# Bidirectional RWKV layer ahead of latent attention: the scan's operands at 1.7 parts per stretch instead of 2.4, the POOL work beside its inverses on DVE, and the first two attention weight tiles in a pool of their own

## The chip, the cores and the metric

One core of one Trainium2 chip runs the whole program in one launch. The metric is the device time of one execution in microseconds; the time before is 4227.73 us, the median of 3 runs (4226.45 to 4228.69). The engines are called PE (TensorE, matmuls), DVE (VectorE), ACT (ScalarE), POOL (GpSimd) and SP (the queue from which most DMAs are issued).

## The reference, cut to what matters

The network has two blocks. The first (two hybrid attention layers with their feed-forward parts) is not touched. The second has four layers on 512 tokens and 256 context tokens, 1024 wide: a gated mixer, an RWKV-7 layer, latent attention, and a gated mixer again. The change lies in the RWKV layer and at the start of the latent attention.

```python
def rwkv7_scan(state0, r, decay, k_dir, v, kk, a, emit):
    ...
    def step(S, inp):
        w_t, k_t, v_t, kk_t, a_t = inp[:5]
        s_kk = jnp.einsum('nbhvk,nbhk->nbhv', S, kk_t)
        S = S * w_t[..., None, :] - s_kk[..., :, None] * (kk_t * a_t)[..., None, :] + v_t[..., :, None] * k_t[..., None, :]
        y_t = jnp.einsum('nbhvk,nbhk->nbhv', S, inp[5]) if emit else None
        return S, y_t
    ...
    y = ys[0] + jnp.flip(ys[1], axis=1)

def rwkv7_output(y, r, k_dir, v, z, r_k, ln_gain, ln_bias, w_out):
    ...
    yn = ((yh - mean) * lax.rsqrt(var + RWKV_LN_EPS)).reshape(y.shape) * ln_gain + ln_bias
    ...
    out = (yn + jnp.sum(bonus, axis=0).reshape(y.shape)).astype(z.dtype)
    return (out * jax.nn.silu(z)) @ w_out

def mla_project(h, w_in, q_norm, kv_norm, w_uq, w_ukv, qk_gain_q, qk_gain_k, need_q):
    ...
        c_q, c_kv, k_rope, z = jnp.split(h @ w_in, [...], axis=-1)
```

The scan runs over 768 tokens (the context's state feeds the latent tokens) in two directions, for 16 heads of 64.

## The kernel before, in words

**Precision.** A full-precision product is three passes (`strip`, L160): each weight tile `wraw` is split into a high part `whi` (L138, ACT) and a low part `wlo` (L141, on DVE, and on POOL at every third tile), and the activations likewise (`split`, L177 on ACT and L178).

**The order of work.** PE's instructions stand in the order in which the Python generators emit them. DVE, ACT, POOL and SP are ordered ahead of time by a scheduler in the compiler, and then each runs its list strictly in order, so an instruction that waits holds everything behind it on its engine.

**The features of the RWKV layer** (`features`). PE makes 32 strips: the eight 128-wide tiles of k, then r, z and v. A strip is eight contraction tiles of 512 + 256 columns and is cut in four stretches; a stretch has pace 1, in the two strips where one kind gives way to the next 0.4. Beside the strips run four side generators, each with a rate: the lora products, `operands` (rate `OPS`, L1185), `by_tokens` and `first`. After each stretch a generator earns its rate times the stretch's pace, and for each whole credit it emits one part.

**The operands.** `operands(f)` (L1571) exists for f = 0 to 7, one for every two heads, and is about 16 parts. A part early on emits the products of the decay and rate loras on PE (L1603, read by ACT in L1604) and the norm's rows (L1264). Then for each of the two directions: kd (L1618, POOL), L1619 and the running sum L1625 (DVE), the exponentials (ACT), and the tiles `st_bk` and `st_ar` (L1645 on POOL, L1646, L1647 and L1649 on DVE), written to DRAM. Some parts later `within` (L1668) multiplies them on PE (L1679) and stores the 32 x 32 blocks that `inverse` reads. `by_tokens(f)` waits until operand set f is done.

**The inverses.** `inverse(k)` (k = 0 to 7, one for each operand set) inverts 96 triangular blocks of 32 x 32 in 31 steps of two instructions (L1819, L1821). `first` (L1473) runs inverse 0 on DVE beside the v strips, then `merge(0)`; when all operand sets are done it closes their pool, makes the masks and starts inverse 1 on POOL. Inverses 2 to 7 follow on POOL during the scan. Each ends with stores to DRAM (L1829), which `merge(k)` (L1832) reads back into `TT`; its first matmuls are L1854.

**The scan.** For each k, 12 steps (`step`, L1885 to L1920) form one period; within period k the products and the merge of k + 1 and the output of k - 1 are interleaved on PE. `output` (L1933) normalises `yacc`, adds `ld_b` on POOL (L1959), multiplies by the gate on DVE (L1961), splits it (L177 on ACT, L178 on POOL) and multiplies by two 128 x 512 tiles of `rwkv_w_out_2`. In `step`, DVE copies `rh` (L1892) and the lower half of `VU`, updates `st` (L1908) and writes `SV` (L1915), each between two small matmuls.

**The latent attention's start** (`Mla.run`). A weight pool is opened for the projections; the first two weight tiles `wkv` (128 x 1024) are asked from it ahead of the layer's normed input `hidden` (L978, L979), and the first strip uses both.

Of the kernel before, what the change touches and what calls it, by code (L numbers as in the profile page):

```python
# [16 lines left out]
ALU = mybir.AluOpType  # L17
# [1099 lines left out]
CH = 64  # L1117
# [64 lines left out]
OW = (0.0, 0.4, 1.0)  # L1182
BANKS = (4, 4)
PACE = 0.4
OPS = 2.4  # L1185
WT = 3


class Rwkv:
# [32 lines left out]
    def work(self, tag, shape, bufs, k=0):  # L1222

        at = {"T12": 1, "TT": (3, 2, 0)[k % 3]}.get(tag)
        if at is None:
            return (self.op if tag[:3] == "inv" and tag != "invW" else self.ap).tile(shape, F32, tag=tag, name=tag, bufs=bufs)
        return shaped(self.big(at), shape)
# [247 lines left out]
    def first(self):  # L1475

        tc = self.net.tc
        while self.done["xs"] != "v":
            yield
        self.cur = cur = [{} for k in range(KD)]  # L1480
        X = [self.big(2), self.big(3)]
        cut = lambda t, a, n: t[:, a:a + n]
        place = {"invA": [cut(X[0], 0, 1024)], "invT": [cut(X[1], 0, 1024)], "invP": [cut(X[0], 1024, 256)]}
        turn = {}

        def work(tag, shape, bufs, k=0):
            if tag == "T12":
                return self.work(tag, shape, bufs, k)
            turn[tag] = turn.get(tag, -1) + 1
            return shaped(place[tag][turn[tag] % len(place[tag])], shape)  # L1490

        acc = self.net.aux
        for _ in self.inverse(0, cur[0], work, self.net.nc.vector):
            yield
        t = self.big(2)
        place = {"invW": [cut(t, 768, 256), cut(t, 1024, 256)], "TT": [self.big(3)]}
        yield from self.merge(0, cur[0], work, acc)

        while self.done["op"] < KD:
            yield  # L1500
        self.right.close()
        self.op = self.right.enter_context(tc.tile_pool(name="rwc", reuse_waits="tile", bufs=1, side="right"))
        self.masks(self.op.tile([128, 2, 64], F32, name="rmask"))
        self.slot, self.groups, self.gs = 0, 0, []
        self.steps_to_come = self.ahead(cur)
        inv = self.inverse(1, cur[1], self.work, self.net.nc.gpsimd)
        for _ in range(9):
            next(self.steps_to_come)
            for _ in range(2):
                next(inv)  # L1510
                yield
        yield from inv
# [319 lines left out]
    def merge(self, k, cur, work, acc):  # L1832

        net, nc, ap = self.net, self.net.nc, self.ap
        mt = cur["mt"]
        TA = cur["TT"] = work("TT", [128, 2, NS, CH], 1, k)
        T12 = work("T12", [128, 2, 24, 32], 1)
        T1, M = T12[:, 0], T12[:, 1]
        TF = TA.rearrange("p d s t -> p (d s) t")
        for e in range(2):  # L1840
            nc.sync.dma_start(M[64 * e:64 * e + 32], self.mo[k][e])
            nc.sync.dma_start(T1[64 * e:64 * e + 32], self.blocks(mt[1], e, 0))
            for h in range(2):
                q = 64 * e + 32 * h
                nc.sync.dma_start(TF[q:q + 32, :, 32 * h:32 * h + 32], self.blocks(mt[0], e, h))
            nc.gpsimd.memset(TF[64 * e + 32:64 * e + 64, :, 0:32], 0.0)
        for _ in range(8):
            yield
        for g in range(3):
            pw = acc()  # L1850
            for x in range(8):
                for e in range(2):
                    a, bq = slice(64 * e, 64 * e + 32), slice(64 * e + 32, 64 * e + 64)
                    nc.tensor.matmul(pw[bq, x * 32:x * 32 + 32], lhsT=M[a, g * 8 + x, :], rhs=T1[a, g * 8 + x, :],  # L1854
                                     start=True, stop=True, tile_position=(64 * e, 64 * e + 32))
            yield
            W = work("invW", [128, 8, 32], 2)
            for e in range(2):
                bq = slice(64 * e + 32, 64 * e + 64)
                nc.scalar.copy(W[bq].rearrange("p a b -> p (a b)"), pw[bq, :256])  # L1860
            yield
            pz = acc()
            for x in range(8):
                for e in range(2):
                    a, bq = slice(64 * e, 64 * e + 32), slice(64 * e + 32, 64 * e + 64)
                    nc.tensor.matmul(pz[a, x * 32:x * 32 + 32], lhsT=W[bq, x, :], rhs=TF[bq, g * 8 + x, 32:64],
                                     start=True, stop=True, tile_position=(64 * e + 32, 64 * e))
            yield
            for e in range(2):
                a = slice(64 * e, 64 * e + 32)  # L1870
                nc.scalar.activation(TF[a, g * 8:g * 8 + 8, 32:64], pz[a, :256].rearrange("p (x c) -> p x c", c=32), AF.Copy, scale=-1.0)
            yield
# [60 lines left out]
    def output(self, k, cur):  # L1933
# [22 lines left out]
        yield  # L1956
        nc.scalar.activation(y, y, AF.Identity, scale=col(P["lg"], k), bias=col(P["lb"], k))
        yield
        nc.gpsimd.tensor_tensor(y, y, bonus, ALU.add)  # L1959
        yield  # L1960
        nc.vector.scalar_tensor_tensor(y, y, 0.5, z, ALU.mult, ALU.mult)  # L1961
        yield
        yh = ap.tile([128, T], F32R, tag="yh", name="yh", bufs=1)
        yl = ap.tile([128, T], F32R, tag="yl", name="yl", bufs=1)
        net.split(yh, yl, y, nc.gpsimd)
        yield
        for f in range(KD):
            if f % 4 == 0:
                hi, lo = net.wtile([(0, net.I["rwkv_w_out_2"][0][rows, f * 128:f * 128 + 512])], 1, 512)
            a, b = net.acc(), net.acc()  # L1970
            outs = [(a, 0, S), (b[:, :C], S, T)]
            net.strip(outs, [(hi[:, 0], lo[:, 0])], [(yh, yl)], c0=f % 4 * 128)
            yield
            self.b2.residual(self.i, f, outs, ap if k == KD - 1 else None)
# [22 lines left out]
class Mla:  # L1997
# [5 lines left out]
    def run(self):  # L2003
# [5 lines left out]
        with ExitStack() as es:  # L2009
# [24 lines left out]
            krt = mp.tile([128, NT2, 64], F32, name="krt")  # L2034
            kr2 = mp.tile([128, NT2], F32, name="kr2")
            with net.weight_pool(2, 3, 2), net.psum(6, 2), tc.tile_pool(name="mla1", reuse_waits="tile", bufs=3) as ap:
                wkv = [net.wcols(w_in[:, 768 + k * 128:896 + k * 128], 128) for k in range(2)]
                hT = self.b2.hidden(i, ap, ap, True)

                raw = [ap.tile([128, T], F32, name=f"ckr{k}", bufs=1) for k in range(2)]  # L2040
# [28 lines left out]
                for h in range(MH):  # L2069
                    ps = net.acc()  # L2070
                    net.strip([(ps, 0, S)], net.wcols(w_in[:, 1088 + h * 128:1216 + h * 128], 128), hT)
                    z = ap.tile([128, S], F32, tag="zs", name="zs", bufs=2)
                    nc.scalar.activation(z, ps, AF.Tanh, scale=0.5)
                    nc.vector.scalar_tensor_tensor(z, z, 1.0, ps, ALU.add, ALU.mult)
                    nc.sync.dma_start(zd[h * 128:h * 128 + 128, :], z)
                    if h == 0:
                        self.normed(rawq, cq, cols["qn"], 768, ((0, NCH),), ap)
            net.drop_context()
            na, nb, nw, no = HEAD_BANKS
            with net.weight_pool(1, 3, 3), net.psum(na, nb, nw), tc.tile_pool(name="po", reuse_waits="tile", bufs=no, space=PSUM) as self.pv, \  # L2080
# [382 lines left out]
```

## Time and profile before

| What | Before |
|---|---|
| Median of 3 runs | 4227.73 us |
| Profiled execution | 4218.81 us |
| Its span | 4216.9 us |
| Mean granted TensorE clock | 0.952 |
| PE busy | 3855.6 us, 91% of the span, 26432 matmuls |
| DVE busy | 2461.7 us, 58% |
| ACT busy | 1545.2 us, 37% |
| POOL busy | 1317.8 us, 31%, 1340 instructions |

The profiled execution lies 8.9 us below the median of the runs. A busy share is a mean over the whole program; the changed places lie between 2134 us and 3092 us of the span, where the share differs from stage to stage. In the rows below, a time is counted from the start of the span, and the granted clock (PEclk) is a share of full speed, averaged over the stretch.

### The profile page before, as it was taken

Reading aid. Unit: us, or ns where it says so; the run is one execution under the profiler, and the core shown is the slowest. Engines: PE = TensorE matmul, PEld = TensorE weight load, DVE = VectorE, ACT = ScalarE, POOL = GpSimd, SP = SyncE. Lnnn points to the kernel's source line nnn. Section 1 sums busy time; section 2 is a strip of 40 time slices with the busy share of each in tenths; the row PEclk is TensorE's granted clock in tenths of the full one; section 3 lists DMA queues with packets and bytes.
Section 4 is the critical chain, followed back from the end, with each engine's and each line's share of the span. In section 5 each row is a group of like instructions: output and inputs, shape, how many; then the busy total and the mean of one; then the engine's idle time right before and its main releaser. Section 6 shows DMA issues by size and latency. Waiting matters only on the chain. (4 is left out here: it accounts for less than half of the span.)

```text
span 4216.9 us, 67232 instructions
## 1 busy us (share of the span) xinstructions
PE 3855.6 (91%) x26432; PEld 3192.2 (76%) x26432; DVE 2461.7 (58%) x4804; ACT 1545.2 (37%) x2945; POOL 1317.8 (31%) x1340
## 2 busy tenths in 40 slices
PE   8999999999999999998887797588789899998999
PEld 7867777787877788887766576477577788887887
DVE  7836445865554434444767644477643778883544
ACT  4243223334332422223454433244343455553222
POOL 3321111322111211113445578820121344442221
PEclk9999999999999999999899898799889999999999
DMA  3125543213364322222257866355223121221332
GB/s 92 51 79 162 175 132 90 61 56 100 103 202 158 102 65 61 60 61 78 70 158 202 226 166 156 91 128 124 79 61 114 51 61 52 61 77 62 93 91 85
DMA packets 599015, 431.72 MB, mean 102 GB/s; under 512 B 193436, under 2 KB 532140, under 8 KB 598700
## 3 DMA queue, kind: packets, MB, share of 16 engines
q1 hardware_dynamic: 593756, 414.97, 34.1%
q0 software_dynamic: 4944, 12.46, 1.2%
q8 instruction: 209, 3.42, 0.3%
q14 instruction: 106, 0.87, 0.1%
HBM read 354.46 MB, written 68.68 MB: 100 GB/s over the span
## 5 line engine op out<-in xcount | busy, mean ns | idle before, releaser
L138 ACT CAST whi<-wraw 128x1024 fp32r<-128x1024 f32 (+3 forms) x471 | 457.5, 972 | 1183.0 <-PE acc L160 971.4
L141 POOL TENSOR_TENSOR wlo<-wraw,whi 128x1024 fp32r<-128x1024 f32 (+2 forms) x205 | 426.9, 2083 | 1291.3 <-ACT whi L138 1182.1
L160 PE MATMUL acc<-hh,whi 128*128 128x512 f32 (+2 forms) x1776 | 625.2, 377 | 9.5 <-ACT hh L421 5.0
L160 PE MATMUL acc<-hl,whi 128*128 128x512 f32 (+2 forms) x1776 | 620.8, 374 | 2.5 <-DVE hl L422 2.5
L160 PE MATMUL acc<-hh,wlo 128*128 128x512 f32 (+2 forms) x1776 | 620.3, 374 | 2.0 <-DVE wlo L141 2.0
L141 DVE TENSOR_TENSOR wlo<-wraw,whi 128x1024 fp32r<-128x1024 f32 (+3 forms) x266 | 330.6, 1244 | 467.1 <-ACT whi L138 420.7
L160 PEld LDWEIGHTS acc<-hh,whi 128*128 128x128 f32 (+1 forms) x1776 | 314.7, 188 | 84.0 <-ACT whi L138 17.3
L160 PEld LDWEIGHTS acc<-hh,wlo 128*128 128x128 f32 (+1 forms) x1776 | 314.4, 187 | 63.4 <-DVE wlo L141 2.8
L160 PEld LDWEIGHTS acc<-hl,whi 128*128 128x128 f32 (+1 forms) x1776 | 314.6, 188 | 62.3 <-DVE hl L422 4.1
L160 PE MATMUL acc<-wlo,hh 128*128 128x256 f32 (+1 forms) x896 | 297.2, 332 | 6.5 <-DVE wlo L141 6.5
L160 PE MATMUL acc<-whi,hh 128*128 128x256 f32 (+1 forms) x896 | 298.1, 335 | 2.9 <-ACT hh L978 2.3
L160 PE MATMUL acc<-whi,hl 128*128 128x256 f32 (+1 forms) x896 | 293.4, 331 | 1.5 <-DVE hl L979 1.5
L999 DVE SCALAR_TENSOR_TENSOR xT<-acc,mod,xT 128x512 f32<-128x512 f32 x256 | 185.6, 746 | 139.6 <-PE acc L160 138.9
L160 PEld LDWEIGHTS acc<-wlo,hh 128*128 128x128 f32 x896 | 179.5, 201 | 20.4 <-DVE wlo L141 7.3
L160 PEld LDWEIGHTS acc<-whi,hh 128*128 128x128 f32 x896 | 179.4, 201 | 20.5 <-ACT hh L978 2.9
L160 PEld LDWEIGHTS acc<-whi,hl 128*128 128x128 f32 x896 | 178.4, 200 | 16.3 <-DVE hl L979 2.4
L160 PE MATMUL wide<-xsh,whi 128*128 128x512 f32 (+1 forms) x512 | 147.4, 371 | 16.5 <-ACT xsh L1384 16.5
L160 PE MATMUL wide<-xsl,whi 128*128 128x512 f32 (+1 forms) x512 | 142.0, 360 | 17.0 <-POOL xsl L1385 13.5
L160 PE MATMUL wide<-xsh,wlo 128*128 128x512 f32 (+1 forms) x512 | 140.0, 356 | 0.0
L160 PE MATMUL acc<-ffgh,whi 128*128 128x512 f32 x352 | 139.9, 400 | 0.0
L160 PE MATMUL acc<-ffgl,whi 128*128 128x512 f32 x352 | 138.4, 395 | 0.0
L160 PE MATMUL acc<-ffgh,wlo 128*128 128x512 f32 x352 | 138.3, 395 | 0.0
(625 smaller groups left out, 8754.9 us busy)
## 6 DMA issues: line engine op xcount, KB each, us to landing
ada_w<-in_ada_w SPq DMA_DIRECT2D x32, 1536.0 KB
wraw<-in_sgu_w_in SPq DMA_DIRECT2D x96, 512.0 KB
wraw<-in_w_up SPq DMA_DIRECT2D x88, 512.0 KB
wraw<-in_w_in SPq DMA_DIRECT2D x44, 512.0 KB
wraw<-in_w_down SPq DMA_DIRECT2D x32, 512.0 KB
wraw<-in_sgu_w_out SPq DMA_DIRECT2D x32, 512.0 KB
wraw<-in_rwkv_w_in SPq DMA_DIRECT2D x32, 512.0 KB
bk<-rw_bk SPq DMA_DIRECT2D x24, 512.0 KB
```

The source lines that it names most:

```text
L138: nc.scalar.copy(hi, raw)
L141: eng.tensor_tensor(lo, raw, hi.bitcast(F32), ALU.subtract)
L160: mm(out, lhsT=a, rhs=b[:, t0:t1], start=first and n == 0, stop=last and n == 2)
L999: nc.vector.scalar_tensor_tensor(dst[k], ps, m[:, 16 + k, j:j + 1], dst[k], ALU.mult, ALU.add)
```

## The change

1. `OPS` goes from 2.4 to 1.7, so the 128 or so parts of the eight operand sets are spread over more stretches of the features.
2. In `output`, three uses of POOL become uses of DVE: the sum with `ld_b` (L1959), the low part `yl` (L178), and the low parts of the two weight tiles (`nc_lo`), five of sixteen of which stood on POOL.
3. `merge` cleared two pieces of a new `TT` with POOL for every k (L1846, 16 memsets); now three tiles are kept in turn and cleared once each, on DVE.
4. The attention's two first weight tiles come from a pool of their own, "mlw", on the right side of the memory, which is closed after the projections.

```diff
-OPS = 2.4
+OPS = 1.7
...
         self.cur = cur = [{} for k in range(KD)]
+        self.tts = []
...
-        TA = cur["TT"] = work("TT", [128, 2, NS, CH], 1, k)
+
+        if k < 3:
+            self.tts.append(work("TT", [128, 2, NS, CH], 1, k))
+        TA = cur["TT"] = self.tts[k % 3]
...
-            nc.gpsimd.memset(TF[64 * e + 32:64 * e + 64, :, 0:32], 0.0)
+            if k < 3:
+                nc.vector.memset(TF[64 * e + 32:64 * e + 64, :, 0:32], 0.0)
...
-        nc.gpsimd.tensor_tensor(y, y, bonus, ALU.add)
+        nc.vector.tensor_tensor(y, y, bonus, ALU.add)
...
-        net.split(yh, yl, y, nc.gpsimd)
+        net.split(yh, yl, y)
...
-                hi, lo = net.wtile([(0, net.I["rwkv_w_out_2"][0][rows, f * 128:f * 128 + 512])], 1, 512)
+                hi, lo = net.wtile([(0, net.I["rwkv_w_out_2"][0][rows, f * 128:f * 128 + 512])], 1, 512, nc_lo=nc.vector)
...
+                own = net.wp, net.wbufs
+                early = ExitStack()
+                net.wp, net.wbufs = early.enter_context(tc.tile_pool(name="mlw", reuse_waits="tile", bufs=1, side="right")), (1, 2, 2)
                 wkv = [net.wcols(w_in[:, 768 + k * 128:896 + k * 128], 128) for k in range(2)]
+                net.wp, net.wbufs = own
...
+            early.close()
             net.drop_context()
```

A line of the changed kernel has a number that is 1 to 11 higher than in the kernel before. The first place where the order moves is POOL at the start of inverse 1. Before, the list reads as follows (`st_bk` is the last operand set's, `rmask` and `G` belong to the scan's masks, `xsl` is an activation's low part for a v strip):

```order
L1645 TENSOR_TENSOR st_bk<-kd,tmp 128x12x64
L1233 MEMSET rmask 128x128
...
L1812 MEMSET invT 96x1024
L1385 TENSOR_TENSOR xsl<-xs,xsh 128x768
L1813 MEMSET invT 96x32
L1385 TENSOR_TENSOR xsl<-xs,xsh 128x768
L1813 MEMSET invT 96x32
L1819 TENSOR_TENSOR invP<-invA,invT 96x31
L141 TENSOR_TENSOR wlo<-wraw,whi 128x1024
L1821 TENSOR_TENSOR invT<-invT,invP 96x31
```

Now the same place reads:

```order
L1646 TENSOR_TENSOR st_bk<-kd,tmp 128x12x64
L1233 MEMSET rmask 128x128
L1761 MEMSET G_20323 64x8x64 x2
L1811 DMA invA<-rw_md_16218 96x1024
L1813 MEMSET invT 96x1024
L1237 AFFINE_SELECT rmask<-rmask 64x64 x4
L1811 DMA invA<-rw_md_16219 96x1024
L1813 MEMSET invT 96x1024
L1814 MEMSET invT 96x32 x2
L1820 TENSOR_TENSOR invP<-invA,invT 96x31
L1822 TENSOR_TENSOR invT<-invT,invP 96x31
```

The `xsl` and `wlo` instructions no longer stand between the steps of an inverse: the last operand set comes after the last `xsl`, and from there on POOL's list is the seven inverses one after the other.

The second place is DVE during inverse 0. Before, only two `wlo`, the copies `rst` and the inverse's own steps stand in it; now the last operand sets do too:

```order
L1822 TENSOR_TENSOR xx_19351<-xx_19351,xx_19350 96x5x27
L1647 TENSOR_TENSOR st_ar<-eb,ld_r 128x12x64
L1820 TENSOR_TENSOR xx_19350<-xx_19350,xx_19351 96x112
L1822 TENSOR_TENSOR xx_19351<-xx_19351,xx_19350 96x4x28
L1820 TENSOR_TENSOR xx_19350<-xx_19350,xx_19351 96x87
L1822 TENSOR_TENSOR xx_19351<-xx_19351,xx_19350 96x3x29
L1820 TENSOR_TENSOR xx_19350<-xx_19350,xx_19351 96x60
L1611 SCALAR_TENSOR_TENSOR kq<-ld_k,col_rwkv,aux 128x512
L1611 SCALAR_TENSOR_TENSOR kq<-ld_k,col_rwkv,aux 128x256
```

Here `xx` is inverse 0's working tile, and L1611 and L1647 belong to the last operand sets; before, all L1611 and L1647 of the eight sets stood ahead of the first step of inverse 0.

The third place is the first output of the scan. On POOL before, its two instructions stand inside inverse 6 (13x19 and so on are the sizes of its steps):

```order
L1821 TENSOR_TENSOR invT<-invT,invP 96x13x19
L1819 TENSOR_TENSOR invP<-invA,invT 96x240
L1959 TENSOR_TENSOR yacc<-yacc,ld_b 128x768
L1821 TENSOR_TENSOR invT<-invT,invP 96x12x20
L1819 TENSOR_TENSOR invP<-invA,invT 96x231
L1821 TENSOR_TENSOR invT<-invT,invP 96x11x21
L178 TENSOR_TENSOR yl<-yacc,yh 128x768
```

On DVE now, between the small instructions of the scan's steps:

```order
L1960 TENSOR_TENSOR yacc<-yacc,acc 128x512
L1960 TENSOR_TENSOR yacc<-yacc,acc 128x256
L1903 COPY VU<-aux 64x2x64
L1964 TENSOR_TENSOR yacc<-yacc,ld_b 128x768
L1903 COPY VU<-aux 64x2x64
L1913 SCALAR_TENSOR_TENSOR st<-st,rw_ec,aux 128x64 x2
L1966 SCALAR_TENSOR_TENSOR yacc<-yacc,ld_z 128x768
L1920 TENSOR_TENSOR SV<-st,rw_ec 64x2x64
L1913 SCALAR_TENSOR_TENSOR st<-st,rw_ec,aux 128x64 x2
L1920 TENSOR_TENSOR SV<-st,rw_ec 64x2x64
L178 TENSOR_TENSOR yl<-yacc,yh 128x768
```

L1964 and L178 are the two that stood on POOL; the gate's product (L1961 before, L1966 now) stood and stands on DVE behind the sum with `ld_b`.

## Rows read from the trace of the kernel before

**Rows 1.** Busy time by stage: microseconds, engines' busy time, granted clock, DMA.
```profile
core 0: us, PE busy (x) PEld busy (x) DVE busy (x) ACT busy (x) POOL busy (x), PEclk, DMA share, GB/s
2134.00:2407.00 273.00, 212.47 (x1682) 171.76 (x1681) 191.75 (x160) 140.17 (x211) 139.62 (x83) 0.91 0.75 203
2407.00:2541.00 134.00, 114.43 (x813) 94.33 (x812) 65.75 (x104) 38.08 (x66) 104.75 (x168) 0.91 0.67 184
2630.00:2735.00 105.00, 52.79 (x887) 43.80 (x887) 43.34 (x129) 22.77 (x70) 92.81 (x163) 0.72 0.39 88
2795.00:2957.00 162.00, 144.65 (x2652) 119.55 (x2650) 119.92 (x387) 68.62 (x211) 16.38 (x12) 0.98 0.54 127
3041.00:3092.00 51.00, 26.11 (x109) 21.02 (x109) 27.32 (x67) 18.64 (x31) 16.19 (x15) 0.64 0.17 52
```

**Rows 2.** Lines of PE, 2134 to 2407 us: busy, mean ns, idle before them.
```profile
line engine op names shapes xcount | busy us, mean ns | idle before us <-releasers
L1679 PE MATMUL aux<-st_ar,st_bk 64*64 64x64 f32 x768 | 32.6, 252 | 40.6 <-DVE st_bk L1647 40.6
L1603 PE MATMUL aux<-ha,a 64*128 64x512 f32 (+1 forms) x64 | 15.0, 515 | 4.0 <-ACT tmp L1604 4.0
L1603 PE MATMUL aux<-hw,w 64*128 64x512 f32 (+1 forms) x64 | 14.9, 589 | 0.0
L1264 PE MATMUL aux<-ident,hs_rep 128*128 128x128 f32 x48 | 9.2, 328 | 15.9 <-ACT tmp L1604 15.9
```

**Rows 3.** Lines of DVE, 2407 to 2541 us: the steps of inverse 0.
```profile
L1821 DVE TENSOR_TENSOR xx<-xx,xx 96x31 f32<-96x31 f32 (+15 forms) x31 | 17.9, 578 | 1.0
L1819 DVE TENSOR_TENSOR xx<-xx,xx 96x31 f32<-96x31 f32 (+15 forms) x31 | 17.4, 563 | 1.0
```

**Rows 4.** Waits by engine, 2630 to 2735 us: total, times, longest.
```profile
engine line waited for: us in total, times, longest us
PE aux L1885 <- DVE rh L1892: 44.3, 1, 44.3
ACT yh L177 <- DVE yacc L1961: 44.3, 1, 44.3
DVE yacc L1961 <- POOL yacc L1959: 43.1, 1, 43.1
```

**Rows 5.** Timeline of that wait's end: start, duration, instruction, idle before.
```profile
start us, us, engine line op out<-in xcount [idle before <-releaser]
2691.78 1.80 POOL L1959 TENSOR_TENSOR yacc<-yacc,ld_b 128x768 f32<-128x768 f32 x1
2693.61 1.43 DVE L1961 SCALAR_TENSOR_TENSOR yacc<-yacc,ld_z 128x768 f32<-128x768 f32 x1 [43.12 <-POOL yacc L1959]
2695.30 1.12 PE L1885 MATMUL aux<-rh,xx 64*64 64x64 f32 x16 [44.29 <-DVE rh L1892]
```

**Rows 6.** Waits of PE, 2735 to 2795 us.
```profile
PE aux L1885 <- DVE SV L1915: 5.7, 2, 5.3
```

**Rows 7.** Timeline of a later output, with no inverse running.
```profile
2808.51 1.82 POOL L1959 TENSOR_TENSOR yacc<-yacc,ld_b 128x768 f32<-128x768 f32 x1 [17.10 <-ACT yacc L1957]
2810.91 0.95 DVE L1961 SCALAR_TENSOR_TENSOR yacc<-yacc,ld_z 128x768 f32<-128x768 f32 x1
2812.80 1.81 POOL L178 TENSOR_TENSOR yl<-yacc,yh 128x768 fp32r<-128x768 f32 x1 [2.47 <-ACT yh L177]
```

**Rows 8.** DVE's line L1915, 2570 to 2650 us, then 2795 to 2957 us.
```profile
L1915 DVE TENSOR_TENSOR SV<-st,rw_ec 64x128 f32<-64x128 f32 x17 | 9.2, 541 | 0.6
...
L1915 DVE TENSOR_TENSOR SV<-st,rw_ec 64x128 f32<-64x128 f32 x33 | 11.2, 363 | 0.8
```

**Rows 9.** Timeline of POOL: inverse 1's load, the ends of inverses 2, 3, 4.
```profile
2401.72 0.59 POOL L1810 DMA_DIRECT2D invA<-rw_md  x1
...
2530.62 0.56 POOL L1829 DMA_DIRECT2D rw_mt<-invT  x1
2577.18 0.55 POOL L1829 DMA_DIRECT2D rw_mt<-invT  x1
2620.45 0.56 POOL L1829 DMA_DIRECT2D rw_mt<-invT  x1
```

**Rows 10.** Timeline of PE: the scan's first full step, merges of 1 and 2.
```profile
2540.61 0.45 PE L1885 MATMUL aux<-rh,xx 64*64 64x64 f32 x8 [0.70 <-DVE rh L1892]
...
2571.34 1.06 PE L1854 MATMUL acc<-xx 32*32 32x32 f32 x32
...
2613.02 0.69 PE L1854 MATMUL acc<-xx 32*32 32x32 f32 x32
```

**Rows 11.** Waits of PE, 3082 to 3200 us: the latent attention's first strip.
```profile
PE acc L160 <- ACT whi L138: 4.5, 1, 4.5
...
PE acc L160 <- DVE wlo L141: 2.0, 1, 2.0
```

## The prediction

> **What bounds the kernel now.** I read the page's head first: PE is busy 91% of the span and every other engine far less, so only places where PE waits are worth anything. The busy times by stage show where that is [rows 1]. In the strips r and z (2134 to 2407 us) PE is busy 212.5 of 273.0 us; in the v strips (2407 to 2541) 114.4 of 134.0; in the scan's stretch 2630 to 2735 only 52.8 of 105.0; once no inverse runs (2795 to 2957) 144.7 of 162.0. DVE is never full in any of them (at most 191.8 of 273.0), and POOL is nearly full in the scan's stretch alone (92.8 of 105.0). The granted clock falls where PE waits (0.72 in that stretch, 0.98 later), so a stall that goes gives back a little beyond itself.
>
> The lines of PE in r and z say what it waits for [rows 2]: 40.6 us in front of the products of the operands (L1679), which wait for DVE's `st_bk`; 15.9 and 4.0 us in front of L1264 and L1603, which wait for ACT's turn over their PSUM tiles. That is 60.5 us for eight operand sets, 7.6 us each. The list of waits in the scan shows one hole of 44.3 us [rows 4], and the timeline gives its end [rows 5]: POOL's L1959 runs at 2691.78, DVE's L1961 behind it, and 0.2 us after that PE starts L1885. POOL runs its list in order and L1959 stands between the steps of inverse 6, with 35 of its 62 instructions ahead; DVE, in order too, waits with L1961 and holds `rh` behind it. So the scan stands still until POOL has come as far as that in its inverses.
>
> **The change part by part.** The sums are made against the profiled execution's own 4218.8 us; the median of the runs is 8.9 us above it, and I add my difference to the median.
>
> *1. OPS 1.7.* About 16 parts for each of 8 sets are 128 parts; at 2.4 for each of four stretches they take 128 / 9.6 = 13.3 strips, at 1.7 18.8 strips. In the order of PE the groups of L1603 move accordingly: eight of them stand in the r and z strips now, six after, and two stand in the first v strips; the last L1679 goes from the seventh z strip to the fifth v strip. Between a set's L1603 and its first L1679 lie 7 to 8 parts: 0.8 strip before, 1.2 strips after, that is 17 us x 0.35 = 6 us more for the chain ACT, DVE, `st_bk` (273.0 / 16 = 17.1 us a strip [rows 1]). The 40.6 us are made of many waits, not one, so most of them are shorter than that. PE's own work per set is (32.6 + 15.0 + 14.9 + 9.2) / 8 = 9.0 us [rows 2]. It only moves: 18 us leave r and z and come back in v. For the stalls: the six sets that stay keep, I estimate, 3 us each (the ACT part, 15.9 us of 60.5, is not cured by a slower pace), 18 us; the two in the v strips keep the old 7.6 each, 15 us, because DVE there also runs inverse 0 (17.9 + 17.4 = 35.3 us [rows 3]) with the sets' instructions between its steps. 60.5 - 33 = 27 us gained. Bounds: 60, if no stall is left; and a loss of 15, if the stalls stay as they are and DVE in the v strips becomes the limit: its 65.8 us of 134 [rows 1] rise by two sets, 2 x 191.8 / 8 = 48 us at most, to 114 of 152, so it isn't full but has little left. I take -27.
>
> *2. The hole in the scan.* With L1959 and L178 on DVE nothing of the scan waits for POOL inside an inverse any more except the merges. All 43.1 us of L1961's wait [rows 4] go: -43. What is late next is the DVE's own list, where the sum with `ld_b` waits for ACT, not POOL; ACT had long finished there. Of this at least 30 should show even if the next merge holds PE a little.
>
> *3. The next period* has the same wait in small: PE 5.7 us behind `SV` [rows 6], behind L1961: -4.
>
> *4. The other outputs.* Away from inverses L1959 takes 1.82 us and L178 1.81 us on POOL [rows 7]; on DVE I take 0.95 us each, the time of L1961, whose size is the same. The chain from ACT to the first output matmul shortens by 1.7 us in each of the other six periods. The last one (3041 to 3092, PE busy 26.1 of 51.0 [rows 1]) has nothing beside it and gets all of it; in the others PE has scan work to do, and DVE's two more instructions (1.9 us) push `rh` and `SV` back now and then. I take -8 in all; bounds +6 (each of six periods loses 1 us) and -10.
>
> Here the trace speaks against moving work to DVE, and I weigh it: `SV` (L1915, two inputs in SBUF) takes 0.54 us on average while POOL runs inverses and 0.36 us later [rows 8], and L1961 1.43 against 0.95 us [rows 5, 7]. A moved instruction beside an inverse so costs up to 0.5 us more. The inverses will run until some 265 us after the scan's first step (term 5), so eight or ten of the sixteen moved ones run beside them: 5 us. That stands in the bounds of this term and of the next. The Trainium skill (SBUF — State Buffer, section Who interferes with whom) says that a VectorE instruction with two inputs in SBUF contends with a GpSimd instruction that reads SBUF, and that whoever issues first blocks the other fully. By that rule each of the ten could wait out a whole POOL instruction, and a long one at that, rather than 0.5 us; the trace agrees with the contention (0.54 against 0.36 us), and its means bear out the smaller price.
>
> *5. The inverses on POOL.* They start when the last set is done: 139 us ahead of the scan's first full step now (2401.7 against 2540.6 [rows 9, 10]), after the change in the fifth v strip, about three strips or 50 us ahead of it. Undisturbed, one takes 43.3 to 46.6 us (2577.18, 2620.45 and 2530.62 [rows 9]). Counted from the scan's first step, inverse 1 so ends at -5, 2 at +40, 3 at +85, and the merges of 1 and 2 come at +31 and +72 [rows 10], the later ones about 55 us apart as the periods without a hole are (162 / 3 [rows 1]). Each inverse is some 32 to 36 us ahead of its merge, and the distance grows. Seven are hidden, then. What isn't: the loads of `rw_mt` stand on SP's list among the loads of `G`, `SV` and `VU` for the coming period, so an inverse that is late holds those back. I add +5, between 0 and +30 (one inverse each 4 us late).
>
> *6. Memset and weights.* 16 memsets leave POOL and 6 come to DVE ahead of the scan: nothing, since neither engine is the limit there. The attention's first strip waits 4.5 us for its `whi` and 2.0 us for its `wlo` [rows 11]; with a pool of their own the loads and ACT's casts go ahead of the RWKV layer's end, and one `wlo` too. ACT's casts lie beside the output's matmuls. I take -4, between 0 and -6.5.
>
> The sum is -27 - 43 - 4 - 8 + 5 - 4 = -81 us, and 4227.7 - 81 = 4147 us.
>
> **The rivals.** *A: the inverses become the scan's bound.* Counted from the scan they start 90 us later than now, and they run beside a busier DVE. The merge of 7 wants the last one at +72 + 5 x 55 = +347, and stores and loads take some 10 us (estimated from inverse 0's end to its merge). At 61 us each the last comes at -50 + 7 x 61 + 10 = +387, and the scan ends 40 us later: a gain near 40, 4187 us. For it speaks that inverse 1 took far longer than 45 us now (2401.7 to the end of inverse 2, 129 us for two [rows 9]); against it that what stood between its steps, `xsl` and `wlo`, is gone from there.
>
> *B: the stall only moves.* DVE and ACT need the same time for each set, and with two sets in the v strips PE waits there as it did: term 1 is 0, or costs 10 with the clock. Then 4147 + 27 to 37, about 4180 us. For it: the v strips now wait only 19.6 us, so what is new there would show. Against it: r and z have six sets in 16 strips instead of eight, and DVE there falls by a quarter.
>
> *C: slower.* The same chain decides against the whole change from 67 us for an inverse: -50 + 7 x 67 + 10 = +429 is 82 us behind the merge of 7, as much as the change gains. At 70 us it is 103 us behind, 4147 + 103 = 4250 us. The cause would be that DVE's instructions with two inputs and POOL's lock each other out all along. The mean of `SV` beside an inverse says that DVE loses in this; the ends of the inverses, 43.3 us apart with DVE at work, say that POOL doesn't.
>
> *D: more than forecast.* If all 60 us of the operands' stalls go and the clock rises with them: 4147 - 33 = 4114 us.
>
> **How the numbers follow.** The forecast's own case has 0.66 (4125 to 4165 us), A 0.11, B 0.12, C 0.03, D 0.08. The range reaches from D's side to A and leaves out C and the tails: 4105 to 4195 us. Faster by over 0.2% (8.5 us, about what a measurement of this kernel can tell from no change) is every case but C and the worst of A and B together: 0.94; within it 0.03; slower 0.03.
>
> **What would show it.** Right: in the scan no wait of DVE for POOL over 5 us, PE's hole of 44.3 us gone; the wait in front of L1679 under 20 us in r and z; inverse 2 stored before the merge of 2 asks for it. Wrong: PE waiting in front of L1854 or for `G` and `SV` from DMA (A, C), POOL's inverses over 55 us apart; the v strips over 160 us long (B). If the hole of 44 us stays or comes back under another name, the reading of [rows 4, 5] was wrong, and most of the gain with it.

## The result, and the profile after

The changed kernel takes 4156.78 us (median of 4 runs, 4154.41 to 4159.2) against 4227.09 us before: ratio 0.9836, 95% interval 0.9819 to 0.9853, so 62 to 77 us faster. The forecast was 4147 us. Its profiled execution took 4157.4 us (span 4155.7); the two profiled executions stand 61 us apart and the medians 70, since the one of before (4218.81) lay 8.3 us under this median.

To compare stages I cut both traces at the same four instructions: the end of the first r strip, the scan's first full step, its last step, and the attention's first matmul. The lengths between them, each from one profile, with those of the experiments:

| Kernel | features, us | scan, us | end of scan to attention, us |
|---|---|---|---|
| before | 405.9 | 497.2 | 50.9 |
| changed | 377.6 | 463.3 | 46.2 |
| changed, profiled again | 384.0 | 461.5 | 47.4 |
| OPS 1.7 alone | 392.4 | 500.5 | 50.8 |
| output on DVE alone | 405.5 | 456.4 | 50.0 |
| attention's pool alone | 405.4 | 504.6 | 47.6 |
| TT kept, alone | 414.1 | 492.7 | 50.3 |
| changed, OPS 2.4 | 416.3 | 455.6 | 46.2 |
| changed, OPS 2.0 | 394.3 | 458.2 | 46.4 |
| changed, without the pool | 381.0 | 464.4 | 50.5 |
| changed, negation on ACT | 382.0 | 515.6 | 46.7 |
| changed, rw_mt loads on POOL | 378.9 | 474.4 | 47.3 |
| changed, folded | 381.8 | 454.4 | 45.1 |
| changed, folded, again | 383.1 | 459.0 | 45.0 |

Two profiles of the same kernel differ by up to 6.4 us in a stage (377.6 and 384.0 in the features), which bounds what a single profile can say. Two of the profiled executions lie well above the median of their kernel: that of the output alone by 14 us, that of the changed kernel with OPS 2.4 by 9.

Where periods of the scan are numbered below, the first is its first six steps, the second to eighth are twelve steps each, and five steps are left. The third, which had the hole, begins at 2606.05 us in the changed kernel and at 2630.43 before.

In the changed kernel the busy times by stage are these (columns as in [rows 1]: r and z strips, v strips with the time to the first step, the period that had the hole, and two later periods):

```profile
2139.31:2361.95 222.64, 189.55 (x1456) 152.15 (x1457) 158.99 (x136) 113.53 (x170) 109.57 (x63) 0.94 0.73 203
2361.95:2516.91 154.96, 130.65 (x1028) 105.67 (x1026) 87.84 (x134) 62.96 (x108) 84.85 (x104) 0.90 0.76 208
2606.05:2670.25 64.20, 50.72 (x879) 42.55 (x878) 43.50 (x132) 22.71 (x70) 54.08 (x97) 0.87 0.70 152
2727.64:2785.17 57.53, 49.78 (x880) 41.54 (x879) 44.80 (x132) 22.79 (x70) 45.87 (x83) 0.94 0.56 139
2785.17:2843.60 58.43, 51.52 (x880) 43.15 (x879) 41.07 (x132) 22.82 (x70) 0.00 (x0) 0.88 0.54 127
```

PE's idle time in r and z falls from 60.5 to 33.1 us (222.64 - 189.55), and the period with the hole from 104 to 64 us at a clock of 0.87 instead of 0.72. The fifth and sixth periods, the last two rows, took 53.8 and 54.0 us before; they are longer now.

PE's lines in r and z (columns as in [rows 2]):

```profile
L1680 PE MATMUL aux<-st_ar,st_bk 64*64 64x64 f32 x576 | 20.1, 225 | 10.0 <-DVE st_bk L1648 8.0 <-DVE st_ar L1650 2.0
...
L1264 PE MATMUL aux<-ident,hs_rep 128*128 128x128 f32 x36 | 6.6, 305 | 13.7 <-ACT tmp L1605 13.7
```

Six operand sets stand there now (576 of 768 products), and the wait in front of the products is 10.0 us where it was 40.6. The wait for ACT in front of L1264 has hardly changed. Most of the rest of the 33.1 us, 8.7 us, are short waits for the strips' shifted inputs (`xsl` and `xsh`), which r and z did not have before. In the v strips the two other sets wait little:

```profile
L1680 PE MATMUL aux<-st_ar,st_bk 64*64 64x64 f32 x192 | 6.9, 229 | 0.0
L1604 PE MATMUL aux<-hw,w 64*128 64x512 f32 (+1 forms) x16 | 4.9, 599 | 4.4 <-ACT tmp L1681 4.1 <-ACT tmp L1605 0.4
L1264 PE MATMUL aux<-ident,hs_rep 128*128 128x128 f32 x12 | 2.6, 361 | 4.3 <-ACT tmp L1605 4.3
```

POOL starts inverse 1 at 2463.84, 53 us ahead of the first full step (2516.91), and these inverses end 43 to 44 us apart (42.0 to 46.5 over all seven):

```profile
2463.84 0.59 POOL L1811 DMA_DIRECT2D invA<-rw_md  x1
...
2514.62 0.55 POOL L1830 DMA_DIRECT2D rw_mt<-invT  x1
...
2558.28 0.56 POOL L1830 DMA_DIRECT2D rw_mt<-invT  x1
...
2601.76 0.55 POOL L1830 DMA_DIRECT2D rw_mt<-invT  x1
```

What stands where the hole of 44 us was [rows 4, 5] is smaller and of another kind. From the list of waits of the period 2606 to 2670 us:

```profile
PE acc L1775 <- DMA G<-rw_ar: 7.6, 2, 7.1
PE aux L1890 <- DVE VU L1903: 3.1, 3, 1.7
DVE yacc L1964 <- ACT yacc L1962: 0.8, 1, 0.8
```

DVE waits no more for POOL. Where the 7.1 us come from is seen on SP's queue (start, duration, instruction):

```profile
2605.09 0.33 SPq L1846 DMA_DIRECT2D xx<-rw_mt  x1
...
2606.15 1.03 SPq L1846 DMA_DIRECT2D xx<-rw_mt  x1
2607.28 0.47 SPq L1748 DMA_DIRECT2D bk<-rw_bk  x1
2607.86 4.69 SPq L1849 DMA_DIRECT2D xx<-rw_mt  x4
2612.64 1.26 SPq L1758 DMA_DIRECT2D G<-rw_ar  x2
```

The load of `rw_mt` waits for the store that POOL issues at 2601.76; behind it stand `bk`, four more merge loads and then `G`, on which PE's products wait until 2617.10. The list of SP's waits has it as one row:

```profile
SPq L1846 <- DMA rw_mt<-invT: 5.6, 1, 5.6
```

The longest single wait that is left in the scan is another one, 18 us behind the first full step. DVE's list has the low part of the output's first weight tile (`wlo`, L141) ahead of `rh`; `wlo` waits for ACT's cast, and the cast for a load that comes late on SP's queue, so PE waits 11.5 us for `rh`:

```profile
2540.51 4.72 SPq L135 DMA_DIRECT2D wraw<-in_rwkv_w_out  x2
2543.19 0.62 ACT L138 CAST whi<-wraw 128x512 fp32r<-128x512 f32 x1 [16.10 <-DMA wraw<-in_rwkv_w_out]
2543.84 0.99 DVE L141 TENSOR_TENSOR wlo<-wraw,whi 128x512 fp32r<-128x512 f32 x1 [12.02 <-ACT whi L138]
2546.64 0.69 PE L1890 MATMUL aux<-rh,xx 64*64 64x64 f32 x8 [11.54 <-DVE rh L1897]
```

The kernel before has the same wait, a shorter one:

```profile
2567.76 0.69 PE L1885 MATMUL aux<-rh,xx 64*64 64x64 f32 x8 [8.07 <-DVE rh L1892]
```

In the five profiles at OPS 2.4 it is 7.0 to 8.1 us long, in the nine at 2.0 and 1.7 it is 10.6 to 12.3.

The attention's first strip starts 4 to 5 us sooner after the scan; the waits of [rows 11] for `whi` and `wlo` are replaced by short ones for the split input:

```profile
PE acc L160 <- POOL hl L178: 1.7, 2, 0.9
PE acc L160 <- DVE hl L979: 1.5, 2, 0.8
...
```

But the first 400 matmuls behind that start now take longer, 86.4 us instead of 83.6.

### The profile page after: what moved, and what is told of

The parts are those of the page before. It is cut to its first block, busy times and chain, and to the rows that moved or that the text cites. A ratio compares the mean times of both kernels' runs of the same rounds, so it can differ in the third digit from the quotient of the medians.

```text
span 4155.7 us, 67174 instructions
## 1 busy us (share of the span) xinstructions
PE 3855.6 (93%) x26432; PEld 3192.1 (77%) x26432; DVE 2461.4 (59%) x4831; ACT 1543.0 (37%) x2945; POOL 1268.4 (31%) x1303
## 5 line engine op out<-in xcount | busy, mean ns | idle before, releaser
L141 POOL TENSOR_TENSOR wlo<-wraw,whi 128x1024 fp32r<-128x1024 f32 (+2 forms) x200 | 420.7, 2104 | 1431.2 <-ACT whi L138 1326.9
L141 DVE TENSOR_TENSOR wlo<-wraw,whi 128x1024 fp32r<-128x1024 f32 (+3 forms) x271 | 336.3, 1242 | 451.1 <-ACT whi L138 404.3
L160 PEld LDWEIGHTS acc<-hh,wlo 128*128 128x128 f32 (+1 forms) x1776 | 315.1, 188 | 60.5 <-issue 0.8
L160 PE MATMUL wide<-xsl,whi 128*128 128x512 f32 (+1 forms) x512 | 141.5, 359 | 18.3 <-POOL xsl L1385 12.2
```

The costliest lines, as they stand in the source:

```text
L141: eng.tensor_tensor(lo, raw, hi.bitcast(F32), ALU.subtract)
L160: mm(out, lhsT=a, rhs=b[:, t0:t1], start=first and n == 0, stop=last and n == 2)
```

## The experiments

Theory 1 was that the forecast's terms stand by themselves. The rivals were that OPS 1.7 and the move to DVE need each other, and that the later periods lose to late inverses rather than to DVE's two more instructions. Each ratio is to the kernel before, with its 95% interval.

**OPS 1.7 alone.**

```diff
-OPS = 2.4
+OPS = 1.7
```

> The kernel before with OPS 1.7 alone; the output's instructions stay on POOL. Theory 1 (the terms stand by themselves): the features shorten by 28 us (222 us from the end of the first r strip to that of the last z strip instead of 272, the v strips 147 instead of 125), and the hole in the scan stays near its 43 us: by the order of POOL the sum with ld_b now stands in inverse 5, 16 of its instructions in, so the wait is 30 to 40 us, and a second output waits in inverse 6. Total -28 to -40: 4187 to 4199 us. Rival (OPS 1.7 only pays together with the move to DVE): the later inverses hold the output on POOL by as much as the features gain, so the time is 4220 to 4235 us.

Measured: 4205.83 us, ratio 0.9968 (0.9957 to 0.9979), 11 us less by the medians and 13 by the ratio: neither theory's range. The features gained 13.5 us in this profile, and the scan lost 3. Its waits from 2619 to 2790 us:

```profile
DVE yacc L1961 <- POOL yacc L1959: 33.5, 2, 28.3
PE aux L1885 <- DVE SV L1915: 30.5, 2, 29.7
```

The hole is 28 us, and a second of 5 us follows it, since the inverses come later and the output of the next pair also falls among them. So OPS 1.7 alone doesn't shorten the scan.

**The output on DVE alone.**

```diff
-        nc.gpsimd.tensor_tensor(y, y, bonus, ALU.add)
+        nc.vector.tensor_tensor(y, y, bonus, ALU.add)
...
-        net.split(yh, yl, y, nc.gpsimd)
+        net.split(yh, yl, y)
...
-                hi, lo = net.wtile([...], 1, 512)
+                hi, lo = net.wtile([...], 1, 512, nc_lo=nc.vector)
```

> The kernel before with the output's three uses of POOL on DVE alone, OPS stays 2.4. Theory 1: the hole of 43 us goes, and of it 8 to 12 us are given back in the later periods, where DVE's in-order list delays VU: -33 to -40, 4187 to 4194 us, and DVE's wait for POOL in the scan is gone. Rival (the loss in the later periods of the changed kernel comes from the late inverses and their loads on SP, not from DVE's two more instructions): with the inverses as early as before the later periods stay at 54 us, and the time is 4175 to 4182 us.

Measured: 4166.84 us, ratio 0.9886 (0.9869 to 0.9904), 48 us by the ratio. This is most of the change. The time itself is below both ranges, but the kernel before took 4216.84 us beside it; 48 us below 4227 is 4179, in the rival's range. Its reading is right for the greater part: the fourth to seventh periods are 62.8, 55.7, 54.4 and 54.0 us against 60.5, 53.8, 54.0 and 53.2 before. The last three of these lose 3 us, where they lose 10 in the changed kernel and 6 in its second profile. Over the scan DVE waits for ACT, briefly, and PE for `G` hardly more than before (5.7 us there):

```profile
PE acc L1774 <- DMA G<-rw_ar: 6.9, 7, 2.6
DVE yacc L1959 <- ACT yacc L1957: 5.6, 7, 0.8
```

**The attention's pool alone.**

```diff
...
+                net.wp, net.wbufs = early.enter_context(tc.tile_pool(name="mlw", ..., side="right")), (1, 2, 2)
                 wkv = [net.wcols(...) for k in range(2)]
+                net.wp, net.wbufs = own
...
```

> The kernel before with the pool of its own for the attention's first two weight tiles alone. Theory 1: -4 us (0 to -6.5), 4221 to 4227 us, and PE's wait for whi of 4.5 us in the first strip is gone. Rival: no gain, since the casts go ahead of the output's own on ACT and delay them as much: 4227 us, the wait moved to the output of the last head pair.

Measured: 4222.53 us, ratio 1.0015 (1.0006 to 1.0024): 6 us slower, which neither expected. The wait for `whi` did go and the stretch to the attention is 3.3 us shorter, but two losses stand against it. The scan's last five steps take 38.4 us instead of 34.8: as the rival had it, ACT casts one of the attention's weights (at 3019.06) ahead of the output's own `yh` (at 3020.01), and PE waits for that, where it waited 0.2 us before:

```profile
PE acc L160 <- ACT yh L177: 2.1, 1, 2.1
```

And the first 400 matmuls of the attention take 87.7 us instead of 83.6. This second loss goes with the pool in all profiles, if by little in some: 86.4 to 89.5 us in the nine with it, 83.5 to 85.9 in the five without. PE's waits there are 3.1 us instead of 2.0; the rest is longer busy time, whose cause is not shown. Nor is that of the 4 us that the scan loses at its start in this profile.

**The kept TT tiles alone.**

```diff
+        self.tts = []
...
+        if k < 3:
+            self.tts.append(work("TT", [128, 2, NS, CH], 1, k))
+        TA = cur["TT"] = self.tts[k % 3]
...
-            nc.gpsimd.memset(...)
+            if k < 3:
+                nc.vector.memset(...)
```

> The kernel before with the three kept TT tiles and their memsets on DVE alone. Theory 1: nothing (within 4 us): the inverses on POOL end 1.5 us earlier each, and the sum with ld_b stands 43 instead of 38 instructions deep in inverse 6, so the hole is 43 us give or take 3. Rival: the memsets on POOL are part of the hole, because seven inverses ahead of it lose 1.5 us each, so it shrinks by 7 us or more: 4220 us or less.

Measured: 4218.19 us, ratio 1.0001 (0.9993 to 1.0010): nothing, as theory 1 had it. The hole's period is 102.7 us against 104.3. In this profile the features are 8 us longer and the scan 4.5 us shorter than before.

**The changed kernel with OPS 2.4.**

```diff
-OPS = 1.7
+OPS = 2.4
```

> The changed kernel with OPS back at 2.4, all else as changed. Theory (OPS 1.7 is worth the 28 us of the features, less what the later inverses cost in the scan): the ratio to before is that of the output's move alone, 0.989 to 0.991, some 4177 us where before is 4220; the later periods are 54 to 56 us and no product waits for G. So OPS 1.7 is worth 15 to 25 us on top. Rival (OPS 1.7 costs in the scan what it gains in the features, as in its run alone, where it was worth 13 us): 4160 us or less.

Measured: 4178.85 us, ratio 0.9900 (0.9883 to 0.9917). So on top of the other parts OPS 1.7 is worth 22 us by the medians (4178.85 to 4156.78) and 27 by the ratios (0.0064 of 4225 us), about twice what it is worth alone. By the intervals it is 9 to 18 us alone and 17 to 37 on top, so they just touch, and that OPS 1.7 pays better with the rest of the change is likely rather than shown. By the profiles the extra does not come from the scan, which OPS 1.7 lengthens in both cases (by 3 us alone, by 6 to 9 here), but from the features: 13.5 us less alone, 32 to 39 less here (416.3 to 384.0 and 377.6). Why is open. At OPS 2.4 the features take 405.4 to 405.9 us in the three profiles without the kept TT and 414.1 and 416.3 in the two with it, so the partner may be the kept TT rather than the move to DVE; OPS 1.7 with one of them alone was not run.

The scan is 455.6 us here against 463.3, 464.4 and 461.5 at OPS 1.7. The wait for `rh` in front of the output's first weights is 8.1 us here and 11.5 there, and PE's wait for `G` in the whole scan, at OPS 1.7, is

```profile
PE acc L1775 <- DMA G<-rw_ar: 12.2, 7, 7.1
```

and at 2.4

```profile
PE acc L1775 <- DMA G<-rw_ar: 4.1, 5, 1.6
```

**The changed kernel with OPS 2.0.**

```diff
-OPS = 1.7
+OPS = 2.0
```

> The changed kernel with OPS 2.0. Theory (the changed kernel's scan loses 7 us in the third period and 10 in the later ones because SP's in-order list waits for inverses that come late): the inverses start some 20 us earlier against the scan, the 7 us wait for G goes and the later periods come back to 54 or 55 us, a gain of 10 to 15 in the scan against 5 to 15 more stall in front of the operands' products in r and z: 4145 to 4160 us. Rival (the later periods are longer because of DVE's two more instructions): the scan stays as it is and the features lose, 4162 to 4170 us.

Measured: 4159.81 us, ratio 0.9859 (0.9840 to 0.9877). Features and scan lie between those of 1.7 and 2.4 (394.3 and 458.2 us). The exchange is as expected in kind, but the fourth to sixth periods did not come back as far (58.5, 58.3, 56.4), and `G` is still waited for:

```profile
PE acc L1775 <- DMA G<-rw_ar: 10.2, 8, 3.7
```

The intervals of 2.0 and 1.7 overlap; 2.0 is not better.

**The changed kernel without the attention's pool.**

```diff
...
-                net.wp, net.wbufs = early.enter_context(tc.tile_pool(name="mlw", ..., side="right")), (1, 2, 2)
                 wkv = [net.wcols(...) for k in range(2)]
-                net.wp, net.wbufs = own
...
```

> The changed kernel without the attention's pool of its own. Theory 1 (the pool alone was measured at +6 us, and that holds here): 4148 to 4154 us, ratio to the changed kernel 0.998 to 0.999. Rival (here the pool is worth the 4 us that the first strip waited for its weights): 4158 to 4162 us, and PE waits 6 us in front of the first strip again.

Measured: 4155.23 us, ratio 0.9842 (0.9826 to 0.9859), beside 0.9836 and 0.9841 with the pool: no difference that can be told. The wait is back as the rival had it:

```profile
PE acc L160 <- ACT whi L138: 4.5, 1, 4.5
```

The stretch to the attention is 50.5 us instead of 46.2 to 47.4, but the attention's first 400 matmuls then take 83.5 us instead of 86.4 to 87.7.

**The negation on ACT.** Each inverse ends with a negated transpose, 1.95 us on POOL.

```diff
-        if alone:
-            eng.tensor_scalar(A, Tm.rearrange("p i c -> p c i"), -1.0, 1.0, ALU.mult, ALU.mult)
-        else:
-            nc.scalar.activation(A, Tm.rearrange("p i c -> p c i"), AF.Copy, scale=-1.0)
-        queue.dma_start(mt[0], A)
+        nc.scalar.activation(A, Tm.rearrange("p i c -> p c i"), AF.Copy, scale=-1.0)
+        (nc.scalar if alone else queue).dma_start(mt[0], A)
```

> The changed kernel with the last copy of each inverse (the negated transpose, 1.95 us on POOL) on ACT, and its store on ACT's queue. Theory (late inverses hold SP's loads of G): each inverse is 2 us shorter, the third to be merged is stored 6 us earlier, the wait for G of 7 us in the third period falls to 1 to 3 us: a gain of 4 to 10 us, 4147 to 4153. Rival (the wait for G has another cause, or ACT, in order, waits for POOL and holds VU and SV): 4157 us or more.

Measured: 4210.4 us, ratio 0.9968 (0.9956 to 0.9979), 54 us worse than the changed kernel. The rival's second half was right. From 2515 to 2800 us:

```profile
ACT invA L1825 <- POOL invT L1822: 65.7, 6, 17.4
DVE VU L1900 <- ACT VU L1899: 82.8, 22, 18.0
PE aux L1887 <- DVE VU L1900: 57.7, 17, 18.8
```

ACT stands in order behind an inverse, `VU` stands behind that on ACT, and PE waits: the hole that the change removed, made again on another engine.

**The merges' loads on POOL's queue.**

```diff
-            nc.sync.dma_start(T1[64 * e:64 * e + 32], self.blocks(mt[1], e, 0))
+            (nc.gpsimd if k else nc.sync).dma_start(T1[64 * e:64 * e + 32], self.blocks(mt[1], e, 0))
...
-                nc.sync.dma_start(TF[q:q + 32, :, 32 * h:32 * h + 32], self.blocks(mt[0], e, h))
+                (nc.gpsimd if k else nc.sync).dma_start(TF[q:q + 32, :, 32 * h:32 * h + 32], self.blocks(mt[0], e, h))
```

> The changed kernel with the merges' loads of the inverted blocks (rw_mt, merges 1 to 7) on POOL's queue instead of SP's. Theory (in the third period SP's in-order list waits 5.6 us for the store of inverse 3 and holds the loads of bk and G behind it, so PE's products wait 7 us): PE's wait for G from DMA falls from 12.2 us in the scan to under 5, the third period from 64 to 57 or 58 us; POOL loses some 4 us per inverse to issuing, which the distance of the inverses carries: 4146 to 4156 us. Rival (G is late because its own buffer comes free late, or the DMA engines are full): G's wait and the period stay, and POOL's issuing costs up to 10 us: 4157 to 4170 us.

Measured: 4165.33 us, ratio 0.9868 (0.9853 to 0.9883), a time in the rival's range. The mechanism is still as the theory said: the third period is 56.0 us instead of 64.2 and 62.8, and PE's wait for `G` in the scan 4.8 us instead of 12.2. But two periods later (2718 to 2791 us, 73.2 us long) the merge itself waits for its loads, which stand behind other work on POOL:

```profile
PE acc L1859 <- DMA xx<-rw_mt: 10.2, 2, 8.7
```

So SP's waiting load was the cause of the 7.1 us, and this is not the way to be rid of it.

**The folded output.** The layer norm's bias is added to the bonus in the v strips, and gain and sum become one instruction.

```diff
-        nc.scalar.activation(y, y, AF.Identity, scale=col(P["lg"], k), bias=col(P["lb"], k))
         yield
-        nc.vector.tensor_tensor(y, y, bonus, ALU.add)
+        nc.vector.scalar_tensor_tensor(y, y, col(P["lg"], k), bonus, ALU.mult, ALU.add)
...
+        nc.scalar.activation(st, st, AF.Identity, bias=self.P["lb"][:, f:f + 1])
         nc.sync.dma_start(self.d["bonus"][rows, :], st)
```

> The changed kernel with the output's gain and sum in one DVE instruction (the layer norm's bias is added to the bonus beforehand on ACT, in the v strips), so ACT's pass over yacc and DVE's wait for it go. Theory (the loss of the moved output is DVE's in-order wait for ACT with VU held behind it: PE waits 1.66 us for VU once in each period): the longest wait for VU falls under 1.2 us, the chain at the last output shortens by 1.1 us, DVE's busy time stays: a gain of 6 to 14 us, 4143 to 4151 us. Rival (VU waits because DVE is busy, not because it waits for ACT): nothing in the periods, 1 us at the end, and up to 8 us of ACT in the v strips hidden: 4153 to 4158 us.

Measured: 4147.32 us, ratio 0.9826 (0.9808 to 0.9844), in the theory's range, but not for its reason. The gain is in the scan and 1.1 us at its end. PE's waits in the scan:

```profile
PE aux L1891 <- DVE VU L1904: 26.5, 25, 3.1
...
PE acc L1776 <- DMA G<-rw_ar: 4.9, 5, 2.4
```

`VU` is waited for as long as before (27.3 us in the changed kernel, longest 1.9); the wait for `G` is 7 us shorter. SP's list has the same order there, but inverse 3 is stored 82.6 us after the scan's first full step instead of 84.9, and SP's load of it no longer waits (nor in the second profile, 82.9 us). So the theory on `VU` falls, and why the periods are shorter is not settled beyond that. Both kernels once more, side by side:

> The changed kernel once more, beside the folded one, so that the two stand against the same runs of the kernel before: ratio 0.982 to 0.985, some 4157 us where before is 4225.

> The folded kernel once more. If its gain over the changed one is real (the profile has its scan 9 us shorter: 454 against 463), it is 4 to 12 us faster than the changed kernel in the same runs. If it is the spread between chips and runs, within 3 us of it.

Measured: 4153.11 us (0.9841, 0.9826 to 0.9857) for the changed kernel and 4149.26 us (0.9826, 0.9807 to 0.9844) for the folded one. The folded kernel is 4 us faster side by side, and was 9 us under the changed kernel's first median, with intervals that overlap: probably a few us better, not shown.

## Why the prediction was right, step by step

*The whole.* 81 us were forecast and 70 measured, in the range and inside the main case (4125 to 4165 us). What was off is term 4, together with term 5: the two were to give 3 us, and outside the third and fourth periods the scan lost 9.5 us.

*Term 1, the features (-27).* Right in size: 405.9 to 377.6 us is -28, the mean of the profiles at OPS 2.4 against those at 1.7 gives 409 to 383, -27. But I had worked it out as the worth of OPS 1.7 by itself, and alone that took 13.5 us off the features, on top of the other parts 32 to 39: that the mean fits is in part luck. Its parts were less exact, too. The products' wait fell further in r and z than I took (10.0 us), and L1264's wait for ACT stayed, as said. The strips' inputs, which I had left out, cost 8.7 us there. In the v strips the two sets' products waited not at all; what grew there was PE's work and short waits for ACT, and DVE came to 87.8 us of 155, under the bound of 114. Rival B, that the stall only moves, is refuted.

*Term 2, the hole (-43).* 104.3 to 64.2 us is -40, and the output alone on DVE takes somewhat more (60.8 us). The reading of [rows 4, 5] is confirmed from both sides: OPS alone keeps a hole of 28 us where L1959 is still on POOL, and the negation on ACT makes a new one. One count was off: the wait began at 2650.5, in the last 13 us of inverse 5, and of inverse 6 39 of the 62 steps stood ahead of L1959, not 35.

*Term 3 (-4).* 60.5 to 57.4 us, -3.

*Term 4, the other outputs (-8): the sign was wrong.* The periods after those two lost 10 us together (53.8, 54.0, 53.2 to 57.5, 58.4, 55.0), and only the last output may have gained (0.9 us in the run of the output alone). I counted the shorter chain as a gain although PE in those periods isn't waiting for it, and gave DVE's list too little weight. One output's timeline in the changed kernel shows what happens:

```profile
2628.16 0.96 DVE L1964 TENSOR_TENSOR yacc<-yacc,ld_b 128x768 f32<-128x768 f32 x1 [0.83 <-ACT yacc L1962]
2629.15 0.29 DVE L1903 COPY VU<-aux 64x128 f32<-64x128 f32 x1
...
2629.50 0.45 PE L1890 MATMUL aux<-VU,TK 128*64 128x64 f32 x8 [1.66 <-DVE VU L1903]
```

DVE waits 0.83 us for ACT, then adds, with the second half of `VU` behind it, and PE waits 1.66 us. By the run of the output alone this costs 3 us in these three periods, by the changed kernel at OPS 2.4 4 us; the rest comes with OPS 1.7 and its later inverses.

*Term 5, the later inverses (+5).* The mechanism was named and found: 53 us ahead of the scan (50 forecast), ends 42.0 to 46.5 us apart, inverse 3 stored 85 us after the first step (+85 forecast), and SP holding `G` behind a late load. The scan is 6 to 9 us longer at OPS 1.7 than at 2.4. The waits that are longer there are the one for `G`, by 8 us in the scan, and the one for `rh` behind the output's first weights, by 3.5 us, which I had not named. Rival A is this at a larger size; C did not come, since POOL's inverses did not slow down.

*Contention.* Beside inverses `SV` took 0.54 us before; now DVE's moved instructions there take this (2560 to 2640 us, means in ns):

```profile
L1920 DVE TENSOR_TENSOR SV<-st,rw_ec 64x128 f32<-64x128 f32 x18 | 7.1, 396 | 0.6
L178 DVE TENSOR_TENSOR yl<-yacc,yh 128x768 fp32r<-128x768 f32 x1 | 1.3, 1268 | 0.0
L1964 DVE TENSOR_TENSOR yacc<-yacc,ld_b 128x768 f32<-128x768 f32 x1 | 1.0, 959 | 0.8 <-ACT yacc L1962 0.8
```

`yl` (L178) costs 0.31 us more than its 0.96 us away from inverses, the sum with `ld_b` nothing more. That is within the 0.5 us that I took. Three outputs ran beside inverses, not four or five, and their six moved instructions lost 0.7 us in all, where I took 5. While the sum runs, it is POOL's step, started 0.08 us behind it, that takes longer, 1.40 us; the same step took 0.66 us at 2533.50, with no such instruction beside it:

```profile
2628.24 1.40 POOL L1822 TENSOR_TENSOR invT<-invT,invP 96x247 f32<-96x247 f32 x1
```

The Trainium skill (SBUF — State Buffer, section Who interferes with whom) says that the lock on the shared port is exclusive and that the order of issue decides who blocks; the trace agrees. Since POOL's steps take 0.25 to 0.7 us here, there is little to wait for: `yl` (at 2632.69) started 0.27 us into a step of 0.72.

*Term 6, memset and weights (-4).* The memsets are worth nothing, as said. The stretch to the attention is 4.7 us shorter, of which the pool has 3 to 4 (50.5 to 46.2 or 47.4 without and with it), the last output the rest. In the time the pool doesn't show: with it alone the kernel was 6 us slower, without it the changed kernel the same. The term was right up to the attention's first matmul and left out what comes behind it, where the next 400 matmuls lose some 3 us again. So -4 was wrong as the pool's worth, which is nothing that can be told.

## What to carry to other kernels

When an engine with a long static list shares a small instruction with a latency-bound loop, the loop waits for the whole list ahead of it: look for the wait whose releaser is short but whose engine is busy, and give the loop's engines nothing that stands among long work, on ACT as little as on POOL. The parts of a change have to be measured together as well as alone: OPS 1.7 was worth 11 to 13 us alone and 22 to 27 on top of the rest. A gain that is read in front of one instruction has to be followed beyond it: the pool's 4 us were lost again within the next 84 us. A wait moved off an engine is looked for next on the DMA queue that feeds the same loop.

## What was not expected of the hardware

In one place small gaps went with a loss larger than their length, at a lower granted clock. In the sixth period no inverse runs, and PE has the same matmuls as before, yet its busy time is 51.5 us against 48.4. The stretches of the changed kernel (columns as in [rows 1]):

```profile
2785.17:2789.00 3.83, 2.73 (x45) 2.50 (x44) 1.66 (x7) 1.24 (x3) 0.00 (x0) 1.00 0.78 179
2789.00:2797.00 8.00, 6.54 (x70) 5.72 (x68) 4.28 (x19) 2.65 (x9) 0.00 (x0) 0.58 0.69 198
2797.00:2805.00 8.00, 5.66 (x110) 4.91 (x110) 6.58 (x17) 3.90 (x9) 0.00 (x0) 0.93 0.23 69
2805.00:2813.00 8.00, 7.43 (x98) 6.04 (x95) 5.47 (x17) 2.50 (x13) 0.00 (x0) 0.64 0.65 133
```

and of the kernel before at the same place of the period:

```profile
2849.16:2853.00 3.84, 2.74 (x46) 2.51 (x46) 1.67 (x7) 1.24 (x3) 0.00 (x0) 1.00 0.97 154
2853.00:2861.00 8.00, 7.00 (x123) 5.88 (x122) 7.39 (x28) 4.25 (x13) 0.00 (x0) 1.00 0.71 207
2861.00:2869.00 8.00, 5.50 (x85) 4.28 (x86) 4.65 (x12) 3.78 (x13) 3.63 (x2) 0.93 0.59 126
```

In the stretch where the granted clock falls to a mean of 0.58 (most of it at the lower level of 1.2 GHz) PE waits twice, 0.70 and 0.75 us, for `G` from DMA, and it holds 70 matmuls where it held 123 before. Of the 4.4 us that the period lost, 3.1 are added to PE's busy time and 1.3 are idle. In the second profile of the changed kernel the period has 50.0 us of PE busy in 56.8, at a clock of 0.91 instead of 0.88 (before: 0.97). That these two waits alone brought the clock down is not shown: PE also waits 0.68 and 1.66 us for `VU` ahead of the second low stretch (2805 to 2813 us), and before the clock falls too, to 0.85 in the 8 us behind the last row shown.
